# A two-layer hybrid decoder on one core: new places for three steps of the delta rule, split memory pools, and the indexer in half-projection portions

## The chip, the core and the metric

The kernel runs on one core of one Trainium2 chip. A core has a matrix engine (PE in the profile, with its weight loads shown as PEld), a vector engine (DVE), a scalar engine (ACT), a general engine (POOL) and an engine that only issues transfers (SP). Each takes its instructions strictly in the order in which the program lists them for it; between engines only semaphores order the work. The metric is device time in microseconds (us) of one execution; of several runs the median counts.

## The reference, cut to what matters

Input is x (1024 tokens by 1024 features, float32). Two layers follow each other:

```python
for layer in range(2):
    h = rms_norm(x, norm_gain[layer])
    proj = h @ w_in[layer]                       # 9,304 columns, split into the inputs below
    # branch A: sparse attention. Scores of an indexer, the 256 best causal keys of each query are kept
    iscore = sum_h w_i[t,h] * relu(q_i[t,h] . k_i[s])       # 8 index heads of 64
    sel = top_k(iscore, 256);  y_a = softmax(q_a k_a[sel]) v_a * silu(z_a)
    # branch B: gated delta rule. q, k, v go through a causal convolution of 4 taps and silu first
    decay = exp(gc_i - gc_j) (lower triangle);  lower = (kb k^T * decay) below the diagonal
    u, w = solve (I + lower) u = v*beta, (I + lower) w = kb*exp(gc)
    for each chunk:                              # one after the other, with a running state
        v_new = u_c - w_c @ state
        o_c   = q_dec_c @ state + qk_c @ v_new   # q_dec = q * exp(gc)
        state = state * g_tot + k_dec_c^T @ v_new
    y_b = rms_norm(o) * silu(z_b)
    x = x + (sigmoid(g_a) * y_a + sigmoid(g_b) * y_b) @ w_out[layer]
return rms_norm(x, final_gain)
```

Attention has 8 heads of 128 and 2 key heads, the delta rule 8 heads of 128. All results are float32; each projection multiplies numbers that are split into a high and a low part, so that one block of it takes three matmuls for each of 8 slices of the features: 24 matmuls.

## The kernel before, in words

A layer goes through four stages. **Norm and transposes** (`make_h`). **Token phase** (`token_phase`): the index projections and then q, k and v, for 128 tokens at a time (`proj_tokens`, the matmuls of L365), followed by four of the eight gates of branch A, computed with the features on the partitions (`proj_feat`, the matmuls of L388). **Feature phase** (`feature_phase`): for each of 8 heads three projections of 48 matmuls with their convolutions (`conv`: keys "kf", queries "qf", values "vv"), and one head later the 96 matmuls of that head's output gate, so 240 projection matmuls per head once the first has gone through. **Attention** and the output projection follow.

Two kinds of side work run beside the projections. In the token phase `self.beside` is a chain of generators: `index_scores` (transposes L532 and matmuls L545 on PE, relu on ACT, weighted sums on DVE) and then `select`, which finds each query's threshold bit by bit: 31 rounds of counting passes, "Sign" passes on ACT (L596) for four of six blocks of queries and counts on DVE (L578) for the other two, and at the end six masks (L641 to L648), each of them five DVE passes over tiles `t_junk` and `t_run` and a transfer to DRAM. `tick()` is called after each whole projection of 24 matmuls and draws pieces until their costs have used up SHARE.

In the feature phase the delta rule of a head is cut into steps that `plan_head` places by number: step positions AT_... count projection matmuls since the head began, and `planned` issues each step that is due, on PE not ahead of the matmul at which it fell due. For one head the steps are: load the decays `H` (L722, on POOL's queue, 512 KB) and mask them (L723), load the query decays `qe` (L727, the same queue), exponentials on ACT (L734); transposes of keys (L765) and their scaled copy `kdec` (L784); products (L831) that DVE multiplies into `A` and `H` (L833, L834); the inverse of 32x32 blocks (`inverse_blocks`: four transfers to DRAM and four back into the tile `wide`, 31 steps of two DVE operations on `xc`, L938 and L940, four transfers out as `xscr` and four back into `H`, L947, all on SP's queue); then six steps that join the blocks (`inverse_pairs`: three DVE transposes of H into `xf`, L956, then matmuls L965, L972, L979, L985, L991 with DVE and ACT work between them); 23 steps through the eight chunks (`gdn_chunks`); then the norm (L901 to L903 on DVE, which rescales `vb`), and the transposes of the outputs on PE (L909). Steps of three successive heads are under way at once.

Within an engine the order is made before the run by a scheduler, from readiness that it reckons and from priorities; `issue_after(ins)` forbids it to put what a block traces on the engine of `ins` ahead of `ins`. PSUM holds two `acc` banks and one `more` bank for projections, two `tr` banks for transposes and products, two `ch` and one `oc` for the chunks.

SBUF tiles come from pools that are stacked; a new pool's tiles may lie where closed pools lay, and their first writers then wait for the last users there. Before the change the whole token phase's side work has one pool ("tok"), and the feature phase one pool ("feat") in the same place, with the first convolution's tiles at its start. The tile `wide` serves both the query decays of one head and the inverse of another.

## Time and profile before

| | |
|---|---|
| median of 3 runs | 2746.72 us (2743.76 to 2749.48) |
| profiled execution: time of its own | 2755.04 us |
| profiled execution: span from first to last instruction | 2753.4 us |
| PE busy | 2595.2 us, 94% of the span |
| DVE, ACT, POOL busy | 1886.2, 1348.4, 135.4 us |
| mean clock granted to PE | 0.974 of full speed |

The two layers take about the same time: the feature phase's first convolution starts at 359.5 us in the first layer and at 1734.0 in the second; its steady heads, the fourth to the seventh, come in steps of about 85.6 us. A row of the waits reads: waiting engine, its tile and line, the engine, tile and line (or transfer) that ended the wait, total us, how often, the longest. A row of the windows gives for a stretch its length, each engine's busy time with the number of its instructions, the clock granted to PE (1.00 is full speed), the busy share of the transfer engines and GB/s. A row of the timeline gives start, duration, engine, line, operation, out<-in, shape, and in brackets how long the engine was idle just before and what ended that.

### The profile page before, as it was taken

To read this page: it belongs to the slowest core of one execution; us is meant where nothing else is said; L and a number is where in the kernel's file an instruction comes from. 1 tells how busy PE (TensorE), PEld (TensorE's weight loads), DVE (VectorE), ACT (ScalarE), POOL (GpSimd) and SP (SyncE) were. 2 spreads that over 40 slices of the span, in tenths; PEclk is the share of its full clock that TensorE was granted. 3 is DMA by queue.
4 is the path that set the end of the run, shared out by engine and by line. 5 is a ranking of instruction groups with operands and counts; after the bars stand their busy time and mean duration, and the time that the engine had idled before them with its cause. 6 is when DMAs were issued, how large, how long until landed. Compare 5 with 4: busy or idle time off the path is not lost.

```text
span 2753.4 us, 42170 instructions
## 1 busy us (share of the span) xinstructions
PE 2595.2 (94%) x14858; PEld 2134.8 (78%) x14858; DVE 1886.2 (69%) x5082; ACT 1348.4 (49%) x3107; POOL 135.4 (5%) x386
## 2 busy tenths in 40 slices
PE   7999989989999999999999999899999999999998
PEld 7677767777777788898786777677778777888986
DVE  6678967666676663598356779676767666637965
ACT  5579634343333332598135796333434334237962
POOL 0122000000000000000001220000000000000000
PEclk9999999998999999999999999999999999999999
DMA  3123232142333322431411232321332323234223
GB/s 120 47 66 95 81 82 57 42 79 54 63 56 69 57 60 68 153 102 47 152 53 48 65 97 80 82 66 35 84 75 46 67 60 62 64 103 132 88 83 128
DMA packets 285431, 211.35 MB, mean 77 GB/s; under 512 B 72290, under 2 KB 239268, under 8 KB 285220
## 3 DMA queue, kind: packets, MB, share of 16 engines
q1 hardware_dynamic: 280612, 191.88, 24.8%
q0 software_dynamic: 4608, 16.78, 5.0%
q8 instruction: 117, 1.92, 0.3%
q14 instruction: 94, 0.77, 0.1%
HBM read 162.19 MB, written 46.40 MB: 76 GB/s over the span
## 4 chain that ended last, share of the span: by engine, by line
PE 56%; DVE 11%; DMA 7%; issue 3%; ACT 2%; SPq 1%; POOL 0%; DVEq 0%; ACTq 0%; POOLq 0%
PE acc L388 16%; PE more L388 7%; PE acc L365 7%; PE acc L1137 4%; PE wide L1105 4%; PE tr L1128 2%; DMA H<-xscr 2%; PE out L365 2%; DVE xtmp L938 2%; DVE xc L940 2%; PE tr L831 2%; PE out L388 2%; PE tr L765 1%; DVE w_lo L148 1%; DMA wide<-rows 1%
## 5 line engine op out<-in xcount | busy, mean ns | idle before, releaser
L388 PE MATMUL acc<-lo_t,w_hi 128*128 128x512 f32 x1240 | 511.4, 412 | 0.0
L388 PE MATMUL acc<-hi_t,w_hi 128*128 128x512 f32 x1240 | 503.2, 406 | 6.8 <-DVE gate L663 6.1
L388 PE MATMUL acc<-hi_t,w_lo 128*128 128x512 f32 x1240 | 503.7, 406 | 0.0
L147 ACT CAST w_hi<-w_raw 128x512 fp32r<-128x512 f32 (+1 forms) x336 | 201.4, 602 | 417.3 <-PE acc L388 214.6
L148 DVE TENSOR_TENSOR w_lo<-w_raw,w_hi 128x512 fp32r<-128x512 f32 (+1 forms) x336 | 223.7, 669 | 219.8 <-ACT w_hi L147 190.5
L365 PE MATMUL acc<-w_hi,hi_t 128*128 128x512 f32 (+1 forms) x768 | 287.5, 375 | 15.1 <-ACT w_hi L147 10.2
L365 PE MATMUL acc<-w_lo,hi_t 128*128 128x512 f32 (+1 forms) x768 | 286.8, 374 | 2.1 <-DVE w_lo L148 2.1
L365 PE MATMUL acc<-w_hi,lo_t 128*128 128x512 f32 (+1 forms) x768 | 285.2, 371 | 0.0
L388 PEld LDWEIGHTS acc<-hi_t,w_hi 128*128 128x128 f32 x1240 | 236.3, 191 | 57.2 <-DVE gate L663 7.5
L388 PEld LDWEIGHTS acc<-lo_t,w_hi 128*128 128x128 f32 x1240 | 236.8, 191 | 47.7
L388 PEld LDWEIGHTS acc<-hi_t,w_lo 128*128 128x128 f32 x1240 | 236.8, 191 | 45.3
L596 ACT ACTIVATE t_junk<-scores,t_bits 128x640 f16<-128x640 f32 x248 | 198.9, 802 | 29.5 <-DVE t_bits L588 24.7
L388 PE MATMUL more<-lo_t,w_hi 128*128 128x512 f32 x488 | 203.0, 416 | 0.0
L388 PE MATMUL more<-hi_t,w_hi 128*128 128x512 f32 x488 | 199.7, 409 | 1.7 <-ACT kf L749 1.7
L388 PE MATMUL more<-hi_t,w_lo 128*128 128x512 f32 x488 | 198.9, 408 | 0.0
L365 PEld LDWEIGHTS acc<-w_hi,hi_t 128*128 128x128 f32 x768 | 146.8, 192 | 45.6 <-ACT w_hi L147 13.9
L365 PEld LDWEIGHTS acc<-w_lo,hi_t 128*128 128x128 f32 x768 | 147.4, 192 | 28.5 <-DVE w_lo L148 5.3
L365 PEld LDWEIGHTS acc<-w_hi,lo_t 128*128 128x128 f32 x768 | 147.4, 192 | 22.8 <-issue 1.0
L578 DVE TENSOR_SCALAR_CACHE_REDUCE t_junk<-scores,t_bits 128x1024 f16<-128x1024 f32 (+4 forms) x136 | 153.5, 1128 | 4.3
L886 ACT COPY vb<-oc 128x128 f32<-128x128 f32 x128 | 34.1, 267 | 178.1 <-PE oc L885 169.8
L940 DVE TENSOR_TENSOR xc<-xc,xtmp 128x60 f32<-128x60 f32 (+24 forms) x496 | 104.9, 212 | 12.5
L938 DVE TENSOR_TENSOR xtmp<-wide,xc 128x60 f32<-128x60 f32 (+24 forms) x496 | 103.9, 210 | 12.4
(345 smaller groups left out, 5434.2 us busy)
## 6 DMA issues: line engine op xcount, KB each, us to landing
w_raw<-in_w_in_dram SPq DMA_DIRECT2D x272, 256.0 KB
qs<-stage SPq DMA_DIRECT2D x32, 256.0 KB
ya_gate<-gate SPq DMA_DIRECT2D x32, 256.0 KB
H<-rows POOLq DMA_DIRECT2D x16, 512.0 KB, 9.3
wide<-rows POOLq DMA_DIRECT2D x16, 512.0 KB, 7.6
wide<-hscr SPq DMA_DIRECT2D x64, 128.0 KB
yb<-gate SPq DMA_DIRECT2D x32, 256.0 KB
w_raw<-in_w_out_dram SPq DMA_DIRECT2D x32, 256.0 KB
```

Source lines behind the costliest of these rows:

```text
L147: self.nc.scalar.copy(hi, src)
L148: self.nc.vector.tensor_sub(lo, src, hi.bitcast(F32))
L365: nc.tensor.matmul(acc[t][:, :n], a[:, k, ts], ws[k][b][:, :n], start=k == 0 and i == 0, stop=k == KT - 1 and i == 2)
L388: mm = self.nc.tensor.matmul(acc, ws[k // 4][a][:, cs], act[b][:, k, hs], start=k == 0 and i == 0, stop=k == KT - 1 and i == 2)
L578: nc.vector.tensor_scalar(junk[:, :sc[i].shape[1]], sc[i], thr, 0.0, op0=op, op1=OP.add, accum_out=cnt[:, i:i + 1])
L596: nc.scalar.activation(junk[:, :n], sc[i], AF.Sign, bias=f(bits, i), scale=-1.0, accum_out=cnt[:, i:i + 1])
L831: nc.tensor.matmul(pg[:, o0:o0 + P], kf[:, cs], a[:, cs], start=True, stop=True)
L938: nc.vector.tensor_mul(tmp[:, :n, j + 1:], ln[:, None, j, j + 1:].to_broadcast(shape), X[:, :n, j:j + 1].to_broadcast(shape))
L940: nc.vector.tensor_add(X[:, :n, j + 1:], X[:, :n, j + 1:], tmp[:, :n, j + 1:])
L1105: nc.tensor.matmul(ps[:, :w], qt[a][:, i], kt[b][:, g, o:o + w], start=j == 0, stop=j == 2)
L1128: nc.tensor.transpose(pt[:, o:o + P], rows[i][:, j * P:(j + 1) * P], self.ident)
L1137: nc.tensor.matmul(po, a, b[:, cs], start=j == 0 and i == 0, stop=j == t and i == 2)
```

## The change

It has these parts:

1. `tick` takes the matmul behind which it stands, puts what it draws behind that matmul on PE, is called after each half projection (12 matmuls), and keeps what is over or under as a credit. SHARE is 2.0 per half instead of 4.0 per whole projection; a piece of scoring costs 1.5 times as much as before, a piece of selection 1.4 instead of 1.5. The transposes of the next block's index queries are traced two pieces earlier (`later`).
2. The token phase's pool is split: "sel" holds what the selection needs; "tok", on top of it, holds the scoring's tiles and is closed as soon as the scoring has been traced.
3. The feature phase's pool is split into "conv" (the convolution's padded inputs and `kf`), "keys" (`H`, `qe`, `kdec`, `A`, `xc`, `xtmp`) and "feat" (the rest, `qf`, `vv`, `wide`, `xf` among it). The tiles of "conv" now lie where the index projections' results lay, those of "keys" where the scores and the selection's tiles lie, those of "feat" where the scoring's lay. The zeros at the start of the padded inputs are written by DVE instead of POOL.
4. `qe` has a tile of its own; `wide` is used by the inverse alone.
5. The product of the queries with `qe` (L838 before) leaves the inverse's step and becomes a step at 184, 21 matmuls later.
6. The three DVE transposes that open `inverse_pairs` are put behind the last convolution pass traced until then (`self.convolved`).
7. Pairs, chunks, norms and outputs are placed 10 matmuls later (352, 390, 552, 562 and 568 become 362, 400, 562, 572 and 578).

```diff
-SHARE, SEL_COST = 4.0, 1.5
+SHARE, SCORE_COST, SEL_COST = 2.0, 1.5, 1.4
...
-AT_DECAYS, AT_EXP, AT_KEYS, AT_ROW, AT_QUERIES, AT_PRODUCTS, AT_VALUES, AT_PAIRS, AT_CHUNKS, AT_NORMS, AT_OUTPUTS = (
-    80, 118, (100, 106), 138, (142, 147), (151, 155, 159, 163), (204, 210), 352, 390, 552, (562, 568))
+AT_DECAYS, AT_EXP, AT_KEYS, AT_ROW, AT_QUERIES, AT_PRODUCTS, AT_DECAYED, AT_VALUES, AT_PAIRS, AT_CHUNKS, AT_NORMS, AT_OUTPUTS = (
+    80, 118, (100, 106), 138, (142, 147), (151, 155, 159, 163), 184, (204, 210), 362, 400, 562, (572, 578))
...
+def closing(stack):
+    stack.close()
+    yield 0.0
...
-    def tick(self):
-
-        left = SHARE
-        while left > 0 and self.beside is not None:
-            cost = next(self.beside, None)
-            if cost is None:
-                self.beside = None
-            else:
-                left -= cost
+    def tick(self, mm):
+
+        if self.beside is None:
+            return
+        self.credit += SHARE
+        with self.tc.issue_after(mm.ins):
+            while self.credit > 0 and self.beside is not None:
+                cost = next(self.beside, None)
+                if cost is None:
+                    self.beside, self.credit = None, 0.0
+                else:
+                    self.credit -= cost
...
                 evac(t, acc.pop(t)[:, :n])
-                self.tick()
+            if k % 4 == 3:
+                self.tick(mm)
...
+            if k == KT // 2 - 1:
+                self.tick(mm)
         evac(hs, acc)
         self.planned(mm.ins)
-        self.tick()
+        self.tick(mm)
...
-        with tc.tile_pool(name="tok", bufs=1) as p, self.banks(wide=(1, 4)):
-            self.decays(l, p, raw)
+
+        with tc.tile_pool(name="sel", bufs=1) as p, self.banks(wide=(1, 4)), ExitStack() as scoring:
+            ps = scoring.enter_context(tc.tile_pool(name="tok", bufs=1))
+            self.decays(l, ps, raw)
...
-            self.beside = itertools.chain(self.index_scores(l, p, raw, scores), select)
+            self.beside = itertools.chain(self.index_scores(l, ps, raw, scores), closing(scoring), select)
...
+        later = queries(t0)
+        yield SCORE_COST
+        for t in SEL:
+            qh, ql = later
...
-                yield 2 * n / S
+                if i == 1 and t + 1 < T:
+                    later = queries(t + 1)
+                yield SCORE_COST * 2 * n / S
...
-        with tc.tile_pool(name="feat", bufs=1) as p, self.banks(ch=(1, 2), oc=(1, 1), more=(1, 1)):
+
+        with tc.tile_pool(name="conv", bufs=1) as pc, tc.tile_pool(name="keys", bufs=1) as pk, \
+                tc.tile_pool(name="feat", bufs=1) as p, self.banks(ch=(1, 2), oc=(1, 1), more=(1, 1)):
+            self.pk = pk
...
             for a in self.xps:
-                nc.gpsimd.memset(a[:, 0:4], 0.0)
+                nc.vector.memset(a[:, 0:4], 0.0)
...
+        at(AT_DECAYED, lambda: nc.vector.tensor_mul(hd["qf"], hd["qf"], hd["qe"]))
...
-        qe = hd["qe"] = p.tile([P, 32, 32], F32, name="wide", bufs=1).rearrange("p a b -> p (a b)")
+        qe = hd["qe"] = self.pk.tile([P, S], F32, name="qe", bufs=1)
...
         for j in range(3):
-            nc.vector.scalar_tensor_tensor(dst, xp[:, 1 + j:1 + j + S], cw(j), dst, op0=OP.mult, op1=OP.add)
+            self.convolved = nc.vector.scalar_tensor_tensor(dst, xp[:, 1 + j:1 + j + S], cw(j), dst, op0=OP.mult,
+                                                            op1=OP.add).ins
...
     def gdn_inverse(self, p, hd):
 
-        self.nc.vector.tensor_mul(hd["qf"], hd["qf"], hd["qe"])
         with self.tc.high_priority(offset=AHEAD - PLANNED):
...
-        for b in range(3):
-            bs = slice(32 * b, 32 * b + 32)
-            co = 32 if b == 1 else 0
-            nc.vector.transpose(XF[bs, :, co:co + 32], XT[bs, :, bs])
+        with self.tc.issue_after(self.convolved):
+            for b in range(3):
+                bs = slice(32 * b, 32 * b + 32)
+                co = 32 if b == 1 else 0
+                nc.vector.transpose(XF[bs, :, co:co + 32], XT[bs, :, bs])
```

The rows below are the order of instructions on an engine, each with the line of its own version: in the changed kernel the norm's last operation is L930 (before L903), the convolution passes L782 and L786 (L755 and L758), the transposes into `xf` L984 (L956), the first join L995 (L967).

**DVE, the norm of the fourth head of the first layer.** `rs_y`, `rs_t` and `g_ms` belong to the norm whose result is `vb`; `xf<-H` are the transposes that need the next head's inverse back from DRAM. Before:

```order
L141 SCALAR_TENSOR_TENSOR rs_t<-rs_t,g_ms 128x8
L956 STREAM_TRANSPOSE xf<-H 32x8x32
L142 SCALAR_TENSOR_TENSOR rs_y<-rs_t,rs_y 128x8
L956 STREAM_TRANSPOSE xf<-H 32x8x32
L140 TENSOR_TENSOR rs_t<-rs_y 128x8
L141 SCALAR_TENSOR_TENSOR rs_t<-rs_t,g_ms 128x8
L142 SCALAR_TENSOR_TENSOR rs_y<-rs_t,rs_y 128x8
L956 STREAM_TRANSPOSE xf<-H 32x8x32
L903 TENSOR_TENSOR vb<-vb,rs_y 128x1024
```

Now, the norm's end and, further on in the same list, the transposes:

```order
L145 TENSOR_TENSOR rs_t<-rs_y 128x8
L146 SCALAR_TENSOR_TENSOR rs_t<-rs_t,g_ms 128x8
L153 TENSOR_TENSOR w_lo<-w_raw,w_hi 128x512
L147 SCALAR_TENSOR_TENSOR rs_y<-rs_t,rs_y 128x8
L930 TENSOR_TENSOR vb<-vb,rs_y 128x1024
```

```order
L782 SCALAR_TENSOR_TENSOR qf<-xp_3964,feat_786,qf 128x1024
L143 TENSOR_SCALAR g_rk<-g_rk 128x8
L984 STREAM_TRANSPOSE xf<-H 32x8x32
L145 TENSOR_TENSOR rs_t<-g_rk 128x8
L984 STREAM_TRANSPOSE xf<-H 32x8x32
L146 SCALAR_TENSOR_TENSOR rs_t<-rs_t,g_v 128x8
L984 STREAM_TRANSPOSE xf<-H 32x8x32
L147 SCALAR_TENSOR_TENSOR g_rk<-rs_t,g_rk 128x8
L786 SCALAR_TENSOR_TENSOR qf<-xp_3964,qf 128x1024
L145 TENSOR_TENSOR rs_t<-g_rk 128x8
L995 TENSOR_TENSOR y_8054<-ch,g_nc 32x256
```

The transposes stood in the middle of the norm, ahead of its result; now they stand 13 rows behind it, after the third pass of the next head's query convolution.

**DVE, the end of the first layer's selection.** `t_run` and `t_junk` are the masks' tiles, `kf` the first head's keys. Before, the last of six masks (384 wide) was followed by the first convolution:

```order
L643 SCALAR_TENSOR_TENSOR t_junk<-t_run,t_rest_3540,t_junk 128x384
L645 SCALAR_TENSOR_TENSOR t_run<-scores_1071,t_bits_2028,t_junk 128x384
L647 TENSOR_SCALAR t_junk<-t_run 128x384
L148 TENSOR_TENSOR w_lo<-w_raw,w_hi 128x512 x2
L755 SCALAR_TENSOR_TENSOR kf<-xp_3954,feat_786,kf 128x1024 x2
```

Now the convolution stands between the second mask (1024 wide) and the third (640 wide):

```order
L664 SCALAR_TENSOR_TENSOR t_run<-t_junk 128x1024
L665 SCALAR_TENSOR_TENSOR t_junk<-t_run,t_rest_3802,t_junk 128x1024
L153 TENSOR_TENSOR w_lo<-w_raw,w_hi 128x512
L667 SCALAR_TENSOR_TENSOR t_run<-scores_1079,t_bits_2248,t_junk 128x1024
L153 TENSOR_TENSOR w_lo<-w_raw,w_hi 128x512
L669 TENSOR_SCALAR t_junk<-t_run 128x1024
L782 SCALAR_TENSOR_TENSOR kf<-xp_3964,feat_786,kf 128x1024 x3
L663 TENSOR_SCALAR t_junk<-scores_1076,t_bits_2212 128x640
```

Four masks have moved behind the start of the feature phase; the last one now stands beside the second head's key convolution.

**POOL, the start of the first feature phase.** Before, the zeros of the padded inputs (`xp`) stood behind two loads of decays and their masks:

```order
L722 DMA H<-rows 128x8x128 x2
L678 MEMSET xf 128x512
L723 AFFINE_SELECT H<-H 128x1024
L727 DMA wide<-rows 128x8x128
L723 AFFINE_SELECT H<-H 128x1024
L682 MEMSET xp_3953 128x4
L682 MEMSET xp_3954 128x4
```

Now POOL has the loads and masks alone (L749, L750 and L754 were L722, L723 and L727):

```order
L749 DMA H<-rows 128x8x128 x2
L750 AFFINE_SELECT H<-H 128x1024
L754 DMA qe<-rows 128x8x128
L750 AFFINE_SELECT H<-H 128x1024
L754 DMA qe<-rows 128x8x128
```

The zeros have left this list, and the clearing of `xf` has moved ahead of it, among the rotations of the token phase. Both loads of decays still stand ahead of the first mask.

On PE the counts of projection matmuls at which steps stand shift like this in the first layer. The last matmul of the index scores stands behind 636 of the token projections' matmuls instead of 519 (the projections of q, k and v end at 912). Counted from the first convolution, the first head's keys are transposed at 100 instead of 125, its first products stand at 243 instead of 176, its first joining matmul (L965) at 452 instead of 403. In a steady head, counted from its keys' convolution, the output transposes stand at 96 instead of 91 and the joining matmul of the head before at 133 instead of 118.

24 lines of the change are left out of this document (13 added, 11 removed).

## The prediction, as it was put on record

> **What bounds the kernel now.** First the busy time of each engine:
>
> ```profile
> span 2753.4 us, 42170 instructions
> PE 2595.2 (94%) x14858; PEld 2134.8 (78%) x14858; DVE 1886.2 (69%) x5082; ACT 1348.4 (49%) x3107; POOL 135.4 (5%) x386
> ```
>
> PE is the bound. The change takes no matmul away, so it can save only the time in which PE stands still or runs at a lower clock. Next, therefore, the waits that ended PE's idle time, of which these rows bear on the change:
>
> ```profile
> PE tr L909 <- DVE vb L903: 48.2, 12, 6.7
> PE tr L765 <- issue: 18.0, 2, 9.0
> PE ch L965 <- DVE xf L956: 10.7, 4, 4.8
> PE tr L831 <- DVE H L834: 10.2, 2, 5.2
> PE wide L545 <- ACT qi_hi L147: 7.0, 8, 2.3
> PE acc L388 <- DVE gate L663: 6.1, 3, 2.5
> PE wide L545 <- ACT relu L547: 3.7, 6, 1.6
> ```
>
> They sum to 104 us. Third, windows laid from the start of such a wait, for the clock behind it (the steady head between two norms; then stretches after a wait for scoring, for the first keys in the first layer, for the first and the second join, for the first keys in the second layer; and the selection at its densest):
>
> ```profile
> core 0: us, PE busy (x) PEld busy (x) DVE busy (x) ACT busy (x) POOL busy (x), PEclk, DMA share, GB/s
> 781.68:867.27 85.59, 79.89 (x492) 65.58 (x491) 58.45 (x157) 32.85 (x86) 2.83 (x3) 0.96 0.32 60
> 137.02:140.43 3.41, 3.41 (x19) 2.54 (x17) 0.88 (x2) 3.00 (x9) 0.90 (x4) 0.50 0.23 81
> 393.02:403.26 10.24, 4.34 (x15) 3.79 (x16) 9.54 (x13) 4.33 (x6) 0.00 (x0) 0.50 0.20 36
> 481.76:488.59 6.83, 4.42 (x39) 3.25 (x39) 1.90 (x4) 1.18 (x2) 0.00 (x0) 0.50 0.57 134
> 638.78:655.85 17.07, 17.07 (x136) 12.34 (x135) 2.57 (x6) 3.05 (x7) 0.00 (x0) 0.50 0.16 38
> 1768.59:1778.83 10.24, 4.56 (x15) 4.01 (x16) 9.54 (x13) 4.36 (x7) 0.00 (x0) 0.50 0.11 27
> 225.00:300.00 75.00, 73.08 (x317) 59.24 (x317) 61.21 (x184) 71.07 (x161) 10.51 (x48) 1.00 0.33 93
> ```
>
> A wait costs more than itself: PE then works at half clock (0.50) for some microseconds, and half of such a stretch is lost. In the steady head the mean of 0.96 means 0.04 x 85.6 = 3.4 us lost, beside 5.7 us idle at its start.
>
> **The change part by part.** I add up the waits that each edit can touch.
>
> *A, the transposes behind the convolution.* DVE in a steady head, in order of time:
>
> ```profile
> 784.06 0.43 DVE L956 STREAM_TRANSPOSE xf<-H 32x256 f32<-32x256 f32 x1 [5.12 <-DMA H<-xscr]
> 785.63 0.43 DVE L956 STREAM_TRANSPOSE xf<-H 32x256 f32<-32x256 f32 x1
> 786.10 1.23 DVE L903 TENSOR_TENSOR vb<-vb,rs_y 128x1024 f32<-128x1024 f32 x1
> 798.62 0.42 DVE L967 TENSOR_TENSOR y<-ch,g_nc 32x256 f32<-32x256 f32 x1 [0.17 <-PE ch L965]
> 799.82 1.28 DVE L755 SCALAR_TENSOR_TENSOR qf<-xp,feat,qf 128x1024 f32<-128x1024 f32 x1
> ```
>
> and PE around it:
>
> ```profile
> 787.38 1.97 PE L909 MATMUL tr<-ident,vb 128*128 128x128 f32 x8 [5.70 <-DVE vb L903]
> 793.63 0.39 PE L388 MATMUL more<-hi_t,w_hi 128*128 128x512 f32 x1
> 794.33 0.39 PE L388 MATMUL more<-hi_t,w_hi 128*128 128x512 f32 x1
> 797.88 0.69 PE L965 MATMUL ch<-xf,H 32*32 32x32 f32 x32
> ```
>
> DVE stands 5.12 us at a transpose, because the inverse's last transfer has not landed; behind it in the list is L903, and PE waits for that. Without the transposes in between, L903 could start some 6 us earlier and PE would not wait. Nearly all of the 48.2 us are one wait in each of eight heads: 47 / 8 = 5.9 us, with clock 5.9 + 3.4 = 9.3 us, in all 74 us. What is late next is the join, L965, which needs the transposes: they now stand behind the query convolution's third pass. Its end, 799.82 + 1.28 = 801.1, less two operations of L967 that used to stand ahead (2 x 0.42) plus three transposes (3 x 0.43) and two small operations, say 0.35, gives 801.9. PE used to be there at 797.88 and now has 10 matmuls more to do first; matmuls follow each other by (794.33 - 793.63) / 3 = 0.233 us, so it comes at 800.2. The join is late by 0 (if DVE, freed of 6 us, runs ahead as PE does) to 1.7 us, and 1.7 + 3.4 with the clock. I take 1.5 for each of eight: 12. Net **-62**; bounds 33 (5.1 lost again in each head) to 74.
>
> *B, the entry into the feature phase.* POOL there, then the last mask, the first convolution, and PE:
>
> ```profile
> 376.35 1.96 POOL L722 DMA_DIRECT2D H<-rows  x2 [106.93 <-DMA mask<-t_junk]
> 385.15 1.09 POOL L723 TENSOR_SCALAR_AFFINE_SELECT H<-H 128x1024 f32<-128x1024 f32 x1 [6.30 <-DMA H<-rows]
> 389.56 1.09 POOL L723 TENSOR_SCALAR_AFFINE_SELECT H<-H 128x1024 f32<-128x1024 f32 x1 [2.46 <-DMA H<-rows]
> 390.61 0.13 POOL L682 MEMSET xp<- 128x4 f32 x2
> 390.77 1.28 DVE L755 SCALAR_TENSOR_TENSOR kf<-xp,feat,kf 128x1024 f32<-128x1024 f32 x1 [9.30 <-POOL xp L682]
> 386.28 2.46 ACT L734 ACTIVATE H<-H,ngm 128x128 f32<-128x128 f32 x8 [1.66 <-POOL H L723]
> 398.92 1.94 PE L765 MATMUL tr<-ident,kf 128*128 128x128 f32 x8 [9.04 <-issue]
> 359.48 0.50 PE L388 MATMUL acc<-hi_t,w_hi 128*128 128x512 f32 x1 [1.06 <-DVE gate L663]
> ```
>
> PE's wait is called issue, but the chain is plain: the zeros stand on POOL behind two loads and masks, the convolution waits 9.30 us for them, the transposes wait for the convolution. With the zeros on DVE and memory that is free earlier this chain is gone: 18.0 idle and half of 10.24 of clock twice, 28 us in all. The zeros' DVE time is below 1 us. But `H` still lies over the selection's memory, and the selection ends later: its scoring now ends 636 - 519 = 117 matmuls later, 117 x 0.233 = 27 us. The first loads, at 376.35, thus move to about 403; both are in at 389.56 - 376.35 = 13.2 us after the start, then a mask (1.1) and exponentials (2.5): `H` is ready at about 420. The first products now stand at matmul 243, and PE arrives there at 359.5 + 243 x 0.233 = 416 or, with 16 transposes of about 0.25 each (1.94 / 8), 420. I therefore count a new wait of 0 to 6 us with its clock and take 7 in each layer: net **-14**; bounds 0 to 28.
>
> *C, `qe` in a tile of its own.* The first head's join:
>
> ```profile
> 470.32 2.58 SPq L944 DMA_DIRECT2D xscr<-xc  x4
> 479.93 1.23 DVE L838 TENSOR_TENSOR qf<-qf,wide 128x1024 f32<-128x1024 f32 x1 [6.68 <-DMA wide<-rows]
> 481.69 1.81 SPq L947 DMA_DIRECT2D H<-xscr  x4
> 483.60 1.38 DVE L956 STREAM_TRANSPOSE xf<-H 32x256 f32<-32x256 f32 x3 [1.24 <-DMA H<-xscr]
> ```
>
> DVE waits 6.68 us for the query decays in `wide`; the next head's load into `wide` follows it, and SP holds the four loads into `H` behind that until 481.69, although `xscr` was on its way at 470.3 to 472.9. A tile of its own ends this: about 9 us of delay go. Against it, from the products at 243 (176 before) to the join at 452 (403) there are 209 instead of 227 projection matmuls, 18 x 0.233 = 4 us less room. The stake is 10.7 idle and, for the clock, half of 6.83 behind the first join and half of 17.07 behind the second, in all 22. I take **-15**; bounds 0 to 22.
>
> *D, L831 waiting for `H` (10.2).* This is the third head, whose load into `H` must wait until the first head's chunks have read theirs for the last time. By PE's counts that last read moves from 495 to 511 and the products from 581 to 600, so the room stays the same within 3 matmuls, 0.7 us. **0**, bounds 0 to 10 of gain.
>
> *E, scoring in half portions.* L545 waits 7.0 + 3.7 us, since a piece's queries are split by ACT just ahead of it; transposes two pieces earlier and portions of half the size spread that. With half of the stretches behind (3.41 / 2 for each of some four) the stake is 18. I take **-9**; bounds 0 to 18. The Trainium skill, "TensorE: Matmul & The Clock Gate", section "Why this matters for your kernels", lets the clock fall only behind idle times of about 3 us or more. The longest wait here is 2.3 us, and the row 137.02:140.43 behind it shows 0.50, so this trace disagrees; by the page the stake would be the 11 us of idle time alone, and this term 3 us smaller.
>
> *F, the gates.* PE waits 6.1 us for gates on DVE, with masks of the selection between them. The rest of the masks now stands behind the gates. **-5**; bounds 0 to 6.
>
> Edits 5 and 7 are counted in A and C: on a head's PE list nothing is added. The sum: -62 - 14 - 15 - 0 - 9 - 5 = **-105 us**. The profiled execution took 2755.0 us (2753.4 and 1.6 around it), the median of the runs is 2746.7, 8.3 lower. 2755.0 - 105 = 2650 in a profile, and **2642** as a median. With all terms at their better ends (74 + 28 + 22 + 10 + 18 + 6 = 158) it is 2589, at their worse ends (33) 2714.
>
> **The rivals.**
>
> *All waits go and none comes in their place.* For it: DVE is busy 58.45 of 85.59 us in the steady head, so it has room to run ahead; against it, three chains get nearer to PE. That adds A's other 12, B's 14, C's 7, and E's and F's 10 to the gain, 43 us: about 2600.
>
> *The join inherits the norm's wait.* The transposes are tied to the pass that was traced last; if the order holds them, DVE's whole delay moves to L965, which is then late by its upper bound in every head, 5.1 instead of 1.5: 8 x 3.6 = 29 us worse, 2671. For it: PE's own 10 matmuls are 2.3 us, less than the convolution's last two passes. Against it: PE runs 6 us earlier, but so do the convolution's inputs.
>
> *The norm stays late.* If L903's chain is not early enough without the transposes, because DVE first has to finish the key convolution, half of term A stays, 37 to 40 us: 2681. Against it: DVE idled 5.12 us right there.
>
> *Slower: the longer selection blocks the first head.* The selection is bound by ACT, which is busy 71.07 of 75.00 us in the window from 225. Pushed 27 us later by matmul counts, it competes with the feature phase's own ACT and DVE work; each microsecond beyond 420 at which `H` is ready is one that PE waits at the first products, in both layers. It turns the sum from 105 / 2 = 52 us in each layer on; at 60 us late, with all else as forecast, 2642 + 120 = 2762. For it: rates are set by tables, and four of the masks now stand beside convolutions. Against it: a tail of 60 us needs twice the shift that the order shows.
>
> *Nothing.* The waits are real and the order moves them, so for no change losses would have to cancel gains by chance.
>
> **How the numbers follow.** The forecast, 0.52; all waits gone, 0.17; the join late, 0.13; the norm late, 0.08; the selection late, 0.07; nothing, 0.03. The predicted time is the first's, 2642 us. The range is 2592 to 2700: below it lies little of the second case, above it the slower case and the tails of the third and fourth joined with the bounds of B and C. What a measurement of this kernel can tell from no change is about 0.2%, 5 us: faster by more 0.90, within it 0.03, slower 0.07.
>
> **What would show it.** A: no wait of the output transposes for `vb` over 1 us in the steady heads, a head's step of 77 to 80 us in place of 85.6, and the join's wait for `xf` at most 2 us each. B: no idle DVE ahead of the first key convolution, and instead a wait of PE at the first products or for `H`, under 10 us. C: the first head's loads into `H` right behind `xscr`. E: waits of the scoring below 5 us in sum. The forecast is wrong if steady heads still take over 83 us, or if PE waits more than 20 us in one place at the start of a feature phase; then the place of that wait names the rival.

## The result, and the profile after

The changed kernel takes 2676.65 us (median of 4 runs, 2670.79 to 2677.29) against 2748.1 us for the kernel before (median of 4): a ratio of 0.9734, with a 95% interval of 0.9711 to 0.9757. It is 71 us faster; the forecast was 105 us faster, 2642. The profiled execution took 2677.1 us, 78 less than the profiled one of before. Two rows of the page:

```profile
span 2675.4 us, 42126 instructions
PE 2572.3 (96%) x14858; PEld 2117.8 (79%) x14858; DVE 1886.4 (71%) x5086; ACT 1347.6 (50%) x3107; POOL 145.9 (5%) x382
```

PE has the same 14858 matmuls and fewer idle and slow microseconds. Of the waits that ended PE's idle time in the changed kernel, these rows bear on the prediction (waiting engine, tile, line, then what ended the wait; total us, times, longest):

```profile
PE ch L993 <- DVE rs_t L145: 19.2, 8, 3.5
PE tr L859 <- DVE H L862: 10.3, 2, 5.3
PE ch L903 <- ACT g_u L899: 10.0, 2, 5.2
PE tr L793 <- issue: 8.9, 2, 5.0
PE tr L830 <- DVE g_nc L821: 4.9, 2, 3.7
PE acc L397 <- DVE gate L685: 2.3, 3, 0.9
PE ch L993 <- DVE xf L984: 1.5, 1, 1.5
PE tr L936 <- DVE vb L930: 0.6, 3, 0.2
```

The lines have moved: L936 is the output's transposes (L909 before), L993 the first join (L965), L859 the products (L831), L793 the transposes of keys, queries and values (L765), L903 a chunk's update (L876). The 48.2 us of waits for `vb` have become 0.6, as the prediction's part A said, and the waits of the scoring (7.0, 3.7 and 1.5) have no row left; two new ones of 0.9 us each stand at the transposes of the index queries. But eight joins now wait, 20.7 us together (L993 for `rs_t` and `xf`). The rows for `H`, `g_u` and "issue", 29 us, are waits that have taken the place of old ones. The row for `g_nc`, the factors that the squares of the keys give, is new; 3.7 of its 4.9 us stand in the fourth head of the first layer.

A steady head takes 80.9 us from join to join (85.6 before), with the clock in this window still at 0.96; the six such steps of the two layers lie between 78.3 and 83.0:

```profile
core 0: us, PE busy (x) PEld busy (x) DVE busy (x) ACT busy (x) POOL busy (x), PEclk, DMA share, GB/s
769.00:849.90 80.90, 79.33 (x492) 65.02 (x492) 59.08 (x158) 32.97 (x87) 2.83 (x3) 0.96 0.32 64
```

Why the join waits is read along four engines, in order of time (start, duration, engine, line, operation, and in brackets how long the engine was idle and what ended that):

```profile
749.91 0.88 POOL L749 DMA_DIRECT2D H<-rows  x1 [70.97 <-ACT g_u L899]
759.42 1.71 POOL L750 TENSOR_SCALAR_AFFINE_SELECT H<-H 128x1024 f32<-128x1024 f32 x1 [8.62 <-DMA H<-rows]
761.16 1.58 ACT L761 ACTIVATE H<-H,ngm 128x128 f32<-128x128 f32 x5 [3.15 <-POOL H L750]
763.25 0.69 DVE L800 TENSOR_REDUCE g_ssq<-th 128x4 f32<-128x512 f32 x1 [3.08 <-ACT th L799]
767.19 1.28 DVE L782 SCALAR_TENSOR_TENSOR qf<-xp,feat,qf 128x1024 f32<-128x1024 f32 x1
768.47 0.43 DVE L984 STREAM_TRANSPOSE xf<-H 32x256 f32<-32x256 f32 x1
769.04 0.28 PE L993 MATMUL ch<-xf,H 32*32 32x32 f32 x2 [2.98 <-DVE rs_t L145]
```

The load of the next head's decays `H` is issued at 749.9, lands 9.5 us later, is masked on POOL, and only then can ACT take the exponentials. The squares of the keys stand behind five of these in ACT's list, DVE's sums of squares wait 3.08 us for them, two convolution passes follow (the row shows the second), then the transposes, and PE stands 2.98 us at the join. `rs_t` in the wait's name is only the small operation between the first two transposes. By these rows the join did not inherit a full DVE, but a late load; the first experiment tries that.

The entry into the feature phase and the third head, the same view:

```profile
359.97 3.92 DVE L782 SCALAR_TENSOR_TENSOR kf<-xp,feat,kf 128x1024 f32<-128x1024 f32 x3
368.05 1.09 PE L793 MATMUL tr<-ident,kf 128*128 128x128 f32 x4 [3.84 <-issue]
402.80 1.96 POOL L749 DMA_DIRECT2D H<-rows  x2 [148.84 <-DVE kf L786]
412.25 1.09 POOL L750 TENSOR_SCALAR_AFFINE_SELECT H<-H 128x1024 f32<-128x1024 f32 x1 [7.49 <-DMA H<-rows]
538.69 0.88 POOL L749 DMA_DIRECT2D H<-rows  x1 [113.56 <-PE ch L903]
548.30 2.44 ACT L761 ACTIVATE H<-H,ngm 128x128 f32<-128x128 f32 x8 [5.92 <-POOL H L750]
550.66 0.24 ACT L899 COPY g_u<-ch 128x128 f32<-128x128 f32 x1
```

The first convolution no longer waits for POOL, but for DVE: its input was complete at 353.6, and a mask of 1024 columns stands ahead of it on DVE until about 360. Three passes of the next mask, 2.9 us, stand between its third pass and its last. PE has also come to the keys 25 matmuls earlier and still waits, 3.84 us. The first loads of `H` start at 402.8, where the prediction had put them (403), and PE waits 5.3 us at the first products. In the third head ACT stands 5.92 us for its `H`, with `g_u`, which PE needs, behind it in the list: the 10.2 us that PE used to wait at the products there are now 10.0 us of waiting for `g_u`.

### The profile page after: what moved, and what is told of

Its sections match the earlier page's. It is cut to its first block, busy times and chain, and to the rows that moved or that the text cites. A ratio compares the mean times of both kernels' runs of the same rounds, so it can differ in the third digit from the quotient of the medians.

```text
span 2675.4 us, 42126 instructions
## 1 busy us (share of the span) xinstructions
PE 2572.3 (96%) x14858; PEld 2117.8 (79%) x14858; DVE 1886.4 (71%) x5086; ACT 1347.6 (50%) x3107; POOL 145.9 (5%) x382
## 4 chain that ended last, share of the span: by engine, by line
PE 53%; issue 17%; DMA 4%; DVE 3%; ACT 1%; POOL 1%; SPq 0%; DVEq 0%; POOLq 0%; ACTq 0%
PE acc L397 16%; PE acc L373 9%; PE more L397 6%; PE acc L1165 4%; PE wide L1133 4%; PE tr L1156 2%; PE out L373 2%; PE out L397 2%; PE wide L565 1%; PE tr L859 1%; DMA H<-rows 1%; PE tr L793 1%; DMA w_raw<-in_w_out_dram 1%; DMA pr<-vs 1%; PE ch L903 1%
## 5 line engine op out<-in xcount | busy, mean ns | idle before, releaser
L397 PE MATMUL acc<-lo_t,w_hi 128*128 128x512 f32 x1240 | 505.3, 407 | 0.0
L574 DVE SCALAR_TENSOR_TENSOR scores<-relu,w_idx,scores 128x384 f32<-128x384 f32 (+5 forms) x84 | 81.5, 970 | 60.4 <-ACT relu L567 55.5
L899 ACT COPY g_u<-ch 128x128 f32<-128x128 f32 x128 | 34.0, 267 | 164.6 <-PE ch L897 164.5
L967 DVE TENSOR_TENSOR xc<-xc,xtmp 128x60 f32<-128x60 f32 (+24 forms) x496 | 104.2, 210 | 13.1
```

Of the source, the lines that this page charges most:

```text
L397: mm = self.nc.tensor.matmul(acc, ws[k // 4][a][:, cs], act[b][:, k, hs], start=k == 0 and i == 0, stop=k == KT - 1 and i == 2)
L574: nc.vector.scalar_tensor_tensor(sc[:, :n], rel[half][:, :n], wc, sc[:, :n], op0=OP.mult, op1=OP.add)
L899: nc.scalar.copy(u, pu)
L967: nc.vector.tensor_add(X[:, :n, j + 1:], X[:, :n, j + 1:], tmp[:, :n, j + 1:])
```

## The experiments

Each is the changed kernel with the edit shown, unless it says otherwise; times are medians of 4 runs, beside 7 runs of the kernel before on the same chip, whose medians were 2746.8, 2750.8 and 2752.5 in the three groups; between runs of different groups a few us are therefore not to be read.

**The decays' exponentials ten matmuls later**

```diff
-    80, 118, (100, 106), 138, (142, 147), (151, 155, 159, 163), 184, (204, 210), 362, 400, 562, (572, 578))
+    80, 128, (100, 106), 138, (142, 147), (151, 155, 159, 163), 184, (204, 210), 362, 400, 562, (572, 578))
```

> The changed kernel with one number changed: a head's exponentials of the decays H stand at 128 instead of 118, which puts them behind the two squares of the keys in ACT's list of a steady head. In the changed kernel DVE stands 3.1 us at those squares, since ACT stands 3.2 us at the exponentials for the load of H; two convolution passes and then the transposes into xf follow, and PE waits at the join, 20.7 us in all. Theory 1 (the join is late because the load of H, which starts when the last chunks have read the old one and takes 9.5 us, holds up ACT and so DVE): the idle 3.1 us go, PE's waits at the join for DVE fall from 20.7 below 5 us, and with the clock behind them the time falls by 20 to 35 us, to 2642 to 2657. Theory 2 (the tie to the third pass alone makes the transposes late, DVE is simply full): the join's waits stay above 14 us and the time within 2667 to 2682.

Measured: 2657.2 us, ratio 0.9664 (0.9643 to 0.9684), 19.5 us below the changed kernel. Its steady head on ACT and DVE:

```profile
759.31 0.60 ACT L799 ACTIVATE th<-tr 128x512 f32<-128x512 f32 x1 [1.11 <-PE tr L793]
761.54 0.69 DVE L800 TENSOR_REDUCE g_ssq<-th 128x4 f32<-128x512 f32 x1
765.25 2.44 ACT L761 ACTIVATE H<-H,ngm 128x128 f32<-128x128 f32 x8
```

The squares now go ahead of the exponentials, DVE does not wait for them, and behind the fourth head no join waits more than 0.4 us. What is left, 6.2 us, is the fourth head's join in each layer, 5.3 of them in the first; PE's wait for `g_nc` fell from 4.9 to 1.7 us. Theory 1 holds in its mechanism, though not quite in its numbers: the joins still wait 7.8 us in all (below 5 expected), and the gain, 19.5 us, is just under the 20 to 35 it had given.

**The transposes behind the first pass**

```diff
-            self.convolved = nc.vector.scalar_tensor_tensor(dst, xp[:, 1 + j:1 + j + S], cw(j), dst, op0=OP.mult,
-                                                            op1=OP.add).ins
+            ins = nc.vector.scalar_tensor_tensor(dst, xp[:, 1 + j:1 + j + S], cw(j), dst, op0=OP.mult, op1=OP.add).ins
+            self.convolved = ins if j == 0 else self.convolved
```

> The changed kernel with the transposes into xf tied to the first convolution pass instead of the third. In the order they then stand behind the squares' sums and the keys' copies, but ahead of the second and third pass, 2 x 1.2 us earlier. Theory 1 (ACT's wait for the load of H): the idle time of DVE ahead of them stays 3 us, the join's waits fall by at most 2.4 each, from 20.7 to 3 to 6 us, time 2645 to 2662. Theory 2 (the tie): the waits go altogether, below 2 us, and DVE's idle time does not matter, time 2640 to 2655.

Measured: 2675.4 us, ratio 0.9735 (0.9718 to 0.9753), no change. The waits of this run:

```profile
PE ch L993 <- DVE xf L984: 7.7, 7, 4.9
PE ch L1000 <- DVE y L995: 6.1, 7, 1.0
PE ch L993 <- DVE g_rk L142: 3.2, 3, 1.7
```

The join's waits halved (20.7 to 10.9 us), but the two passes that the transposes left behind now stand ahead of the join's next operation on DVE (L995), and PE waits for that instead. Neither theory gave this time, and theory 1 had expected 3 to 6 us of waits at the join. The place of the tie moves the wait by one step; theory 2, by which the waits would have gone, falls.

**Without part A: no tie, no ten matmuls**

```diff
-    80, 118, (100, 106), 138, (142, 147), (151, 155, 159, 163), 184, (204, 210), 362, 400, 562, (572, 578))
+    80, 118, (100, 106), 138, (142, 147), (151, 155, 159, 163), 184, (204, 210), 352, 390, 552, (562, 568))
...
-        with self.tc.issue_after(self.convolved):
-            for b in range(3):
+        for b in range(3):
```

> The changed kernel without the tie of the transposes and without the ten matmuls of delay, so with the transposes inside the norm's chain again: the price of part A beside all the others. The prediction's term for A is 62 us (bounds 33 to 74): time 2710 to 2750, most likely 2739. By what the trace of the changed kernel shows (47 us of norm waits gone, 20.7 us of waits at the join come, clock behind eight heads 27 before and 20 now, in half-clock losses), A is worth about 33: time about 2710. In both, PE's waits for vb come back with 40 us or more and the waits for rs_t and xf at the join go below 5 us.

Measured: 2705.65 us, ratio 0.9847 (0.9828 to 0.9866), 29 us above the changed kernel. The waits for `vb` are back:

```profile
PE tr L936 <- DVE vb L930: 35.0, 11, 6.1
```

These waits are less than the 40 us that both expectations gave. So part A as a whole is worth 29 us, not 62.

**The tie kept, the ten matmuls undone**

```diff
-    80, 118, (100, 106), 138, (142, 147), (151, 155, 159, 163), 184, (204, 210), 362, 400, 562, (572, 578))
+    80, 118, (100, 106), 138, (142, 147), (151, 155, 159, 163), 184, (204, 210), 352, 390, 552, (562, 568))
```

> The changed kernel without the ten matmuls of delay of pairs, chunks, norms and outputs; the tie stays. The prediction held the join to be bound by the convolution's place: PE then comes to it 10 x 0.233 = 2.3 us earlier, and eight heads lose 2.3 each: 19 us slower, 2690 to 2700. Theory 1 (the join is bound by the load of the next H, which can start only when the chunks have read the old one): the load starts 2.3 us earlier too, so the join's wait changes by less than 1 us a head and the time stays within 2670 to 2684.

Measured: 2640.6 us, ratio 0.9609 (0.9583 to 0.9636): 36 us below the changed kernel. Neither expectation had it. The load of `H`, its mask, the exponentials and the steady head in this run (two views):

```profile
737.24 0.88 POOL L749 DMA_DIRECT2D H<-rows  x1 [68.38 <-DMA xscr<-xc]
746.48 1.09 POOL L750 TENSOR_SCALAR_AFFINE_SELECT H<-H 128x1024 f32<-128x1024 f32 x1 [8.37 <-DMA H<-rows]
748.74 0.40 ACT L761 ACTIVATE H<-H,ngm 128x128 f32<-128x128 f32 x1
749.95 0.60 PE L793 MATMUL tr<-ident,kf 128*128 128x128 f32 x4
```

```profile
755.80:832.80 77.00, 76.91 (x493) 63.28 (x492) 59.03 (x158) 32.58 (x87) 2.83 (x3) 1.00 0.34 64
```

`H` is masked at 747.6, before the second group of key transposes (749.95), and ACT does not wait for it here. (The load's bracket names a transfer of the inverse, which came last; the last chunk's copy `g_u` had ended at 736.9, and the loads of the next two heads name `g_u`, as in the changed kernel.) A steady head takes 77.0 us, PE is busy for 76.9 of them and the clock stays at 1.00. Counting projection matmuls in the two traces: the load is issued 205 matmuls into the preceding head here and 215 in the changed kernel, while the join stands at the same matmul in both within one, since it is bound by the third pass and not by its number. The ten matmuls thus moved only the chunks, and with them the moment at which the last chunk lets go of `H`. Against the run without part A, this one is 65 us faster: that is the tie alone.

**The chunks alone back at 390**

```diff
-    80, 118, (100, 106), 138, (142, 147), (151, 155, 159, 163), 184, (204, 210), 362, 400, 562, (572, 578))
+    80, 118, (100, 106), 138, (142, 147), (151, 155, 159, 163), 184, (204, 210), 362, 390, 562, (572, 578))
```

In this kernel a head's first chunk is placed before its last joining step, so it uses a block that is not yet joined; the amount of work is the same.

> The changed kernel with the chunks alone back at 390 (400); pairs, norms and outputs stay ten matmuls later. Theory 5: what the ten matmuls cost is the load of the next H, which starts when the last chunk has read the old one; it begins 205 matmuls into the preceding head without the shift and 215 with it, while the join stands at the same matmul in both. Then the chunks alone bring the whole gain: 2641, 2635 to 2650, and a load at 205 again. Rival: the later pairs, norms or outputs cost the time (they lengthen the chain from the inverse to the output); then it stays at 2665 to 2680.

Measured: 2640.6 us, ratio 0.9604 (0.9576 to 0.9632), with the load at 205 again. The whole cost of the ten matmuls lies in the chunks, as theory 5 says. Of these 36 us the later exponentials had given back 19.5. About 9 of the rest stand at the fourth head's join of the first layer: 5.3 us of waiting and 13.65 us at half clock with the later exponentials, 2.1 us and none without the ten matmuls. The remaining 7 were not traced to a row.

**Part A on the kernel before**

The tie and the ten matmuls, put into the kernel before.

> The kernel before with part A alone: the tie to the third convolution pass and the ten matmuls of delay. The prediction's term for A is 62 us (33 to 74): 2747 - 62 = 2685. By the changed kernel without A, which was 29 us above the changed kernel, and by its waits at the join (20 us), A is worth about 30 also here: 2710 to 2722. In both the waits for vb go, 47 us of them; the join's waits for DVE then are below 12 us by the prediction and 18 to 28 us by theory 1.

Measured: 2723.9 us, ratio 0.990 (0.9858 to 0.9942): 27 us faster than the kernel before, where the prediction's term said 62. The joins wait 17.1 us for `rs_t` in its profiled execution too (2707.4 us, 16.5 below the median). Within the interval, 16 to 39 us, part A is worth as much here as beside the other parts.

**The shared tile again**

```diff
-        qe = hd["qe"] = self.pk.tile([P, S], F32, name="qe", bufs=1)
+        qe = hd["qe"] = p.tile([P, 32, 32], F32, name="wide", bufs=1).rearrange("p a b -> p (a b)")
...
-        at(AT_DECAYED, lambda: nc.vector.tensor_mul(hd["qf"], hd["qf"], hd["qe"]))
...
     def gdn_inverse(self, p, hd):
+        self.nc.vector.tensor_mul(hd["qf"], hd["qf"], hd["qe"])
```

> The changed kernel with qe sharing the tile of the inverse again and the product of the queries with qe back ahead of the inverse; all else stays. In its order the first head's products fall back from matmul 243 to about 175 and its join from 452 to 403, as in the kernel before, since the other tiles move by 4 KB over the selection's memory. The prediction's term C: 15 us slower than the changed kernel (0 to 22), 2677 to 2699, with the wait at the first joins for xf back (10 us), since the second head's load into the shared tile waits for the query decays of the first. Rival: the tile of its own costs as much at the entry as it gives, because it pushes the keys' tiles over scores that are freed last; then PE's waits at the first products for H (10.3) go and the time stays within 2665 to 2680.

Measured: 2721.2 us, ratio 0.990 (0.9875 to 0.9925), 45 us above the changed kernel, three times the term. The waits of this run:

```profile
PE acc L397 <- ACT qf L775: 16.5, 1, 16.5
PE more L397 <- ACT qf L775: 15.9, 1, 15.9
PE ch L993 <- DVE xf L984: 10.3, 3, 5.1
```

The 10 us at the joins of the first and the third head are back, and something new. ACT, which writes the first head's queries, stands 14.5 us until the transfer of a mask has ended. Without the 4 KB of `qe`, by this reading, these queries lie over the end of the selection's memory; the next run tests it.

**The shared tile, with an unused one of 4 KB in the old place**

```diff
+        self.pk.tile([P, S], F32, name="qe", bufs=1)
         qe = hd["qe"] = p.tile([P, 32, 32], F32, name="wide", bufs=1).rearrange("p a b -> p (a b)")
```

> As the run in which qe shares the inverse's tile again, but with an unused tile of the same 4 KB kept in its place, so that every other tile lies where it lies in the changed kernel. Theory 6: 32 us of that run's 45 were the first queries, whose tile had moved over the end of the selection's memory, so that ACT waited for the last mask; only the rest is the shared tile itself. Then PE's two waits of 16 us for qf are gone and the time is 2680 to 2695. Rival: the shared tile alone costs the 45; then 2715 to 2725.

Measured: 2710.9 us, ratio 0.9858 (0.9824 to 0.9892). The waits for `qf` are gone, as theory 6 says, but the time fell by 10 us and not by 32; neither theory had the size. The row of waits at the first joins, and the windows behind them in the two layers:

```profile
PE ch L994 <- issue: 7.3, 2, 5.4
478.23:498.71 20.48, 19.55 (x140) 14.42 (x141) 9.15 (x12) 4.08 (x8) 0.00 (x0) 0.50 0.19 50
1823.08:1840.15 17.07, 17.07 (x135) 12.40 (x134) 7.01 (x9) 4.16 (x8) 0.00 (x0) 0.50 0.13 34
```

So a wait of 5.4 us at the first join, and 1.9 in the second layer, cost another 19 us in clock (half of 37.55). In the changed kernel the first joins stand in full clock. The tile of its own is thus worth 34 us with all else in its place. Why the waits for `qf` cost only 10 us more, although PE stood 32 us for them, was not tried: the first products stand at another matmul in the two runs, 176 and 243, so the stages behind them differ too.

**The token phase's portions as before**

Side work after each whole projection and not tied to a matmul, the old costs, no credit, the queries' transposes just ahead of their block.

> The changed kernel with the side work of the token phase dealt out as before: after each whole projection, with the old costs, no credit, and the index queries transposed just ahead of their block; all else stays. The selection then ends 27 us of matmuls earlier. Theory 3 (the new waits at the entry, 5.3 and 5.0 us at the first products for H, come from the selection's later end alone): these waits go, while the scoring's waits (13 us before) come back. The prediction's term for the portions is 9 us, and it counted 7 us per layer for the new wait, so by it the time moves between -5 and +5 us, 2671 to 2682. A rival (the first products wait for H whatever the ticks, since two loads and masks stand ahead on POOL): the wait stays above 4 us per layer and the time is 2683 to 2695.

Measured: 2675.2 us, ratio 0.974 (0.9711 to 0.9769), the same time. Its longest row for the scoring, one of the projections of q, k and v, and its first load of `H`:

```profile
PE wide L560 <- ACT qi_hi L152: 7.6, 8, 2.6
PE acc L372 <- ACT stage L420: 5.8, 3, 2.2
```

```profile
376.73 1.96 POOL L742 DMA_DIRECT2D H<-rows  x2 [106.72 <-DVE kf L775]
```

The load starts at 376.7, 26 us earlier, and PE waits neither at the first products nor for the first keys: both rows of the entry, 19.2 us, are gone, and 7.6 us for `g_nc` have come. The scoring waits again, 11.4 us in three rows. So do the projections of q, k and v for their split weights (`w_hi`) and copies (`stage`): five waits of 1.5 to 2.2 us, 9.7 together, where the changed kernel has none over 0.8 (five before, 8.7 together). The gates wait 6.7 us against 2.3. The new portions give and take about the same amount: what scoring, projections and gates gain, the entry loses. That is theory 3 for the wait at the first products, and within the bounds of the prediction's terms.

**The first head later** (with the exponentials at 128)

```diff
+        late = 26 if hd["h"] == 0 else 0
-            at(AT_KEYS[half], lambda half=half: self.gdn_keys(p, hd, half))
+            at(AT_KEYS[half] + late, lambda half=half: self.gdn_keys(p, hd, half))
...
-            at(pos, lambda i=i: self.gdn_products(p, hd, 2 * i))
+            at(pos + 5 * late, lambda i=i: self.gdn_products(p, hd, 2 * i))
-        at(AT_PRODUCTS[-1], lambda: self.gdn_inverse(p, hd))
+        at(AT_PRODUCTS[-1] + 5 * late, lambda: self.gdn_inverse(p, hd))
```

Here the first head's queries are multiplied by `qe` ahead of its products instead of behind them, so its products with the keys contain that factor too; the work is the same.

> The kernel with the later exponentials (128), in which the first head of each layer alone has its keys transposed 26 matmuls later (126) and its products 38 matmuls later (281 instead of 243 in the order). It takes away both new waits at the entry by giving PE other matmuls first: 9.0 us for the first keys and 10.4 us for H at the first products, with 13.7 us of clock behind them. If nothing comes in their place, 2657 - 33 = 2624. The first head's join goes from 452 to 490 and the second's into the crowd at 600, so theory 4 (the first three heads are a chain, what is put off at the entry comes back at the third head, where PE waited 10 us for g_u and 6 us at the join) gives back 10 to 25 us: 2634 to 2650, with waits above 20 us between the third head's products and the first steady head.

Measured: 2673.3 us, ratio 0.9725 (0.969 to 0.9759): 16 us slower than the kernel it starts from. Two rows of it, a wait and a moment on DVE:

```profile
PE tr L831 <- DVE kdec L813: 16.8, 2, 9.2
```

```profile
423.13 1.22 DVE L739 TENSOR_TENSOR qf<-qf,qe 128x1024 f32<-128x1024 f32 x1 [10.38 <-DMA qe<-rows]
```

The old waits are gone, new ones of 17 us for the copies of the keys have come, which stand on DVE behind the last masks and the second head's key convolution, and DVE waits 10.4 us for `qe` with all that is behind it. It gave back more than theory 4 said, and earlier, in the first head itself.

**`H` of the even heads out of the selection's way** (with the ten matmuls undone)

```diff
-        E = hd["H"] = self.pk.tile([P, T, P], F32, name="H", bufs=2)
+        E = hd["H"] = (self.pk if h % 2 else self.pc).tile([P, T, P], F32, name="H", bufs=1)
```

> The changed kernel without the ten matmuls of delay, and with the tile H of even heads taken from the pool of the convolution, which does not reach into the selection's memory. Its first load then needs no wait for the selection, and the first head's products no longer wait for it. Theory 3 (those waits, 5.2 us in each layer, come from the selection's later end through H alone): they go, with half-clock losses of 3.4 each: 2641 - 17 = 2624, 2618 to 2630. Rival: the keys' copies, whose tile still lies over the selection's, and the second head's H hold the same place; then the waits move to them and the time is 2633 to 2645.

Measured: 2638.4 us, ratio 0.9608 (0.9573 to 0.9643), the same as without this edit. The profiled execution took 2651.3 us, 13 more than the median, so its rows serve for places only:

```profile
418.15 1.09 POOL L750 TENSOR_SCALAR_AFFINE_SELECT H<-H 128x1024 f32<-128x1024 f32 x1 [11.31 <-DMA H<-rows]
419.27 2.45 ACT L761 ACTIVATE H<-H,ngm 128x128 f32<-128x128 f32 x8 [9.63 <-POOL H L750]
423.73 1.12 PE L793 MATMUL tr<-ident,vv 128*128 128x128 f32 x4 [5.50 <-ACT vb L877]
```

The first head's `H` is loaded at 257 and its products wait no more. But the second head's `H` still comes at 418, ACT stands at its exponentials for 9.63 us, and the first head's values are behind them in ACT's list: PE waits 5.5 us for those. The rival held.

**And the first head's keys 26 matmuls later**

```diff
+        first = lambda n: n if hd["h"] == 0 else 0
-            at(AT_KEYS[half], lambda half=half: self.gdn_keys(p, hd, half))
+            at(AT_KEYS[half] + first(26), lambda half=half: self.gdn_keys(p, hd, half))
```

> The kernel of the run before with the first head's keys transposed 26 matmuls later in each layer (126), where the convolution is ready. It takes away the wait for the first keys, 8.8 us and some 6.8 of clock. By theory 3 nothing else stands there: 2624 - 15 = 2609. By the rival of the run before, PE now comes earlier to the keys' copies, which the selection's end still holds at 402.7 us, and gives back 4 to 7 us in each layer: 2614 to 2626.

Measured: 2643.95 us, ratio 0.9619 (0.959 to 0.9649), no gain. Its first row of waits:

```profile
PE tr L831 <- DVE kdec L813: 17.1, 2, 9.2
```

The 9.1 us for the first keys are gone and the 2.8 us for their copies became 17.1, more than the rival gave; the copies stand on DVE behind the last mask and the second head's key convolution. In these three runs, moving steps and tiles at the entry only chose where PE waits for DVE's and ACT's work around the end of the selection.

The best of these kernels that computes everything is the changed one without the ten matmuls: 2640.6 us, a ratio of 0.9609 to the kernel before, 36 us below the changed kernel. With `H` of the even heads moved as well it is the same within the interval.

## Why the prediction was right in sign and short in size

The time lies inside the range, 2592 to 2700, and 35 us above the forecast of 2642. Term by term, with idle times from the two kernels' waits and half of the half-clock stretches:

| part | forecast | what the runs show |
|---|---|---|
| A, tie and ten matmuls | -62 | -29: the tie -65, the ten matmuls +36 |
| B, entry | -14 | +5: idle 18.0 to 19.2 (8.9 and 10.3), clock 10.2 to 13.7 |
| C, tile of its own | -15 | -34, with all other tiles in their place |
| D, `H` of the third head | 0 | 0: 10.2 to 10.0, at another instruction |
| E, portions | -9 | about -19: idle 12.2 and four stretches of 3.41 us at half clock, all gone |
| F, gates | -5 | -4: 6.1 to 2.3 |
| sum | -105 | -81, beside -78 between the profiled executions and -71 between the medians |

The measured terms come from different runs and need not add up exactly.

**The step that failed** is the sentence "Edits 5 and 7 are counted in A and C: on a head's PE list nothing is added." It looked at what the ten matmuls do to PE's list, where it is indeed nothing, and not at what the chunks let go of when they end. The trace of before had the link: each load of `H` follows the chunks two heads back, and in the third head, part D, the prediction itself had said that a load "must wait until the first head's chunks have read theirs for the last time". It drew this only for the one place where PE was already waiting. In the steady heads the load had little more than 1 us to spare (masked at 747.6, the exponentials from 748.7 in the run without the shift), and ten matmuls, 2.3 us, used it up. The run with the later exponentials confirms this path for 19.5 of the 36 us, and the run with the chunks alone shows that the rest comes from the chunks too. Of the signs put down for part A, two were missed by this: the step of 80.9 us (77 to 80 forecast) and the longest wait at a join, 3.5 us (2 forecast).

**Part A's mechanism was right and nearly its size.** The tie alone is worth 65 us. The residual wait at the join, for which the forecast took off 12 us, is 2.1 us at one join without the shift: DVE did run ahead as PE does, which had been its better bound.

**B was mis-sized**, and its new wait was rightly placed: `H` came at 402.8 (403 forecast), and PE waited 5.3 us at the first products (0 to 6 forecast). What was missing is the second half: the first convolution was thought free once the zeros had left POOL. But POOL had only been the last of two things to arrive. DVE's masks, which the longer selection had pushed into the same place, came next, with PE 25 matmuls earlier at the keys. The order shown ahead of the prediction had the 1024-wide mask in front of the convolution; its passes were not priced. With the portions as before, the wait for the first keys and the one for `H` are both gone; what the entry lost is thus the price of the selection's later end, and B's own edits did most of what they should.

**C was undersized through the clock**: the waits were right (10 us), but in the run with the unused tile a few microseconds of idle time at the first joins brought 20.5 and 17.1 us of half clock. The forecast had counted 6.83 and 17.07, the second behind what it called the second join; that one, at 638, is the third head's.

**E** took the half of its stake, and the whole of 18 came in: with the waits, the four half-clock stretches in the scoring went too. As the Trainium skill, "TensorE: Matmul & The Clock Gate", section "Why this matters for your kernels", has it, waits under about 3 us would cost no clock, and the term would be the smaller one; the longest of these was 2.3 us, so the trace disagrees with it again. Not counted at all was what the portions do for the waits of the projections of q, k and v themselves: five before, 8.7 us together, of which none over 0.8 us is left.

**The rivals.** "The join inherits the norm's wait", 2671, came closest in time and had the right wait in the right place; its cause, a tie to a full DVE, fell in the run with the later exponentials, where the tie stayed and the waits behind the fourth head's join went. "The longer selection blocks the first head" showed its mechanism, 5.3 and 5.0 us in the two layers, far from the 52 at which it would have turned the sign. "All waits go" is what the run without the ten matmuls approaches, 2640.6, and did not reach, since the entry and the third head kept their waits. "The norm stays late" fell: 0.6 us of waits for `vb` are left.

## What to carry to other kernels

When a step is moved later, ask what it releases at its end, not only what it delays behind it: here ten matmuls on PE moved a 9.5-us load on another queue, and through ACT's and DVE's lists came back to PE as a wait at a join. Where two things arrive at one place nearly together, price the second before claiming the wait for the first. And when the same few microseconds reappear at another line after each edit, as at this kernel's entry, the line is not the cause: look for what ends last (here the selection). Ending it earlier pays only if that costs less elsewhere: with the portions as before it ended 26 us earlier, both waits went, and the time stayed the same.

## What the runs showed of the hardware that was not expected

How little idle time it takes for the clock to fall. Four joins of the changed kernel's steady heads waited 1.5 to 1.8 us. Two of them, with the windows behind:

```profile
849.90 0.22 PE L993 MATMUL ch<-xf,H 32*32 32x32 f32 x2 [1.53 <-DVE rs_t L145]
2088.88 0.22 PE L993 MATMUL ch<-xf,H 32*32 32x32 f32 x2 [1.73 <-DVE rs_t L145]
```

```profile
849.90:856.70 6.80, 6.80 (x102) 4.91 (x102) 5.24 (x19) 3.03 (x7) 0.00 (x0) 1.00 0.17 43
2089.85:2100.09 10.24, 10.24 (x98) 6.98 (x96) 4.75 (x17) 3.48 (x8) 0.00 (x0) 0.50 0.11 28
```

After 1.53 us (and in another head after 1.59) the clock stayed at 1.00; after 1.73 us (and 1.79) it was 0.50 for 10.24 and 6.83 us. So among these four the longer waits cost 3 to 5 us more. But length alone does not decide it. In the run without the ten matmuls a longer wait at the same instruction left the clock at 1.00:

```profile
679.96 0.69 PE L993 MATMUL ch<-xf,H 32*32 32x32 f32 x30 [2.09 <-DVE xf L984]
679.96:686.79 6.83, 6.83 (x114) 5.03 (x115) 5.48 (x20) 1.87 (x5) 0.00 (x0) 1.00 0.16 41
```

In the kernel before, 2.54 us at 335.74 cost no clock either, while 2.27 us at 136.67 did. The half-clock stretches of the changed kernel start whole numbers of steps of 3.41 us apart (those behind its steady joins, at 768.89, 929.32, 2089.85 and 2250.28, lie 47, 340 and 47 steps from each other). So where a wait lies against these marks may decide as much as its length; no run varied that.
